# Mixer weights laid out by pieces on the host, with high and low parts kept together in DRAM

## The chip, the cores and the metric

The kernel is one launch on one core of a Trainium2 chip. A core has a matrix engine (PE, with its weight loads listed as PEld), a vector engine (DVE), an activation engine (ACT), a general engine (POOL) and a queue engine (SP) that here issues every DMA. The metric is the device time of one execution in microseconds, lower is better.

## The reference, cut to what matters

```python
def reference(x, w_in, ..., w_up, w_down):
    h = x                                             # (1, 2048, 1024) float32
    mix = hybrid_mixer(rmsnorm(h, pre_mix_norm), w_in, ..., w_out)
    h = h + rmsnorm(mix, post_mix_norm)
    u = rmsnorm(h, pre_mlp_norm) @ w_up               # 1024 -> 4096
    m = jnp.square(jax.nn.relu(u)) @ w_down           # 4096 -> 1024
    return h + rmsnorm(m, post_mlp_norm)

def hybrid_mixer(h, w_in, ..., w_out):
    z = h @ w_in                                      # 1024 -> 3600 columns, then split
    o_a = chunked_gated_linear_attention(gq, gk, gv, decay from glr)   # 4 heads, dk 64, dv 128
    o_b = chunked_gated_linear_attention(silu(hq), 1 - f, hi, log(f))  # 4 heads, 128 x 128
    return concatenate([gated_norm(o_a, gg), gated_norm(o_b, hg)]) @ w_out
```

All of it is float32 in and out.

## The kernel before, in words

The precision of float32 is had from three fast matmuls. Every operand is split into a high part (`hi`, a rounded copy made on ACT) and a low part (`lo`, raw minus `hi`, on DVE or POOL), and `mm3` (L264) adds `hi*hi`, `hi*lo` and `lo*hi` into one PSUM bank. So lines L267, L268 and L269 come in threes.

The work has three stages. The mixer runs first (0 to about 1010 us): four blocks of 512 tokens, 0 to 3, each a pass over four "units" (pairs of heads, in the order 0, 2, 3, 1) and then the output projection. Then come the up projection (to about 1640 us) and the down projection, which both use a seven-product scheme and read operands that earlier stages stored in DRAM.

The mixer's weights pass through class `Weights` as 72 pieces per block, the same 72 for each block. A piece is 128 partitions by 512 columns (528 for unit 0's values, which carry 16 gate columns). A "chan" piece is four 128x128 squares of `w_in`, a "value" piece is 128 rows of two column ranges of 256 (and the 16 gate columns for unit 0), an "out" piece is 128 rows by 512 columns of `w_out`. `plan` fixes the order in which pieces are taken. `load` issues the DMAs: a raw piece into one of 4 `wr` buffers, at most 4 pieces ahead of the last one that was split (L62). `prep` makes a raw piece into `hi` (tile `w`) and `lo` (tile `wl`), 12 buffers each. In block 0 `prep` splits on ACT (L257) and on DVE or POOL (L258) and stores `lo` to DRAM (`w_low`, L94). In blocks 1 to 3 the raw piece is loaded again (L74), `lo` is loaded from `w_low` (L79) and `hi` is copied anew on ACT (L90).

A matmul group ends in one of 4 PSUM banks `zp`. ACT empties the banks: for values by L498 and L282 (and DVE L500 for the gate columns), for the output projection by L740 and L742. PE can start the next group only when a bank is free.

What sets the order: the kernel is written in program order, and a scheduler then places each engine's instructions by its own simulated time line, so the order on an engine is fixed at build time and each engine runs it strictly in order. An instruction that waits holds up all that stand behind it on its engine. All DMAs stand in one such order, SP's.

`up_raw` (L906) loads a 512x256 half of a group of `w_up` columns, `down_raw` (L1131) a part of `w_down`; both are DMAs with a view that gathers short rows.

Of the kernel before, what the change touches and what calls it, by code (L numbers as in the profile page):

```python
# [38 lines left out]

class Weights:  # L40
# [19 lines left out]
    def load(self):  # L60
        y = self.layer
        while self.loaded < len(self.plan) and self.loaded < self.split + self.RAW:  # L62
            i, kept = self.loaded, self.loaded >= PIECES
            if kept and i >= self.freed + self.LIVE:
                return
            views, chan, _ = self.plan[i]
            raw = y.wp.tile([P, WM], F32, tag="wr", name=y.name("wr"), bufs=self.RAW)
            at = 0
            for v in views:
                n = v.shape[-1] * (4 if chan else 1)  # L70
                dst = raw[:, at:at + n]
                if chan:
                    dst = dst.rearrange("p (k n) -> p k n", n=P)
                y.nc.sync.dma_start(dst, v)  # L74
                at += n
# [4 lines left out]
            self.loaded += 1  # L80

    def prep(self):
        self.load()
# [1373 lines left out]
```

## Time and profile before

| | us |
|---|---|
| median of 3 runs (lowest, highest) | 2303.49 (2301.09, 2305.54) |
| the profiled execution, its own time | 2301.36 |
| its span, first to last instruction | 2299.6 |
| PE busy | 2227.0 (97%) |
| ACT busy | 1170.7 (51%) |
| DVE busy | 1414.0 (61%) |
| DMA moved | 419.20 MB, 182 GB/s over the span |

PE is busy for 97% of the span, so the span is PE's work plus about 72 us in which PE stood still. Most of these stand at the two ends of the span. The rest are waits of a few microseconds each, and the granted clock shows what each leaves behind: after some of them PE runs at less than its full clock for some microseconds.

### The profile page before, as it was taken

To read this page: it belongs to the slowest core of one execution; us is meant where nothing else is said; L and a number is where in the kernel's file an instruction comes from. 1 tells how busy PE (TensorE), PEld (TensorE's weight loads), DVE (VectorE), ACT (ScalarE), POOL (GpSimd) and SP (SyncE) were. 2 spreads that over 40 slices of the span, in tenths; PEclk is the share of its full clock that TensorE was granted. 3 is DMA by queue.
4 is the path that set the end of the run, shared out by engine and by line. 5 is a ranking of instruction groups with operands and counts; after the bars stand their busy time and mean duration, and the time that the engine had idled before them with its cause. 6 is when DMAs were issued, how large, how long until landed. Compare 5 with 4: busy or idle time off the path is not lost.

```text
span 2299.6 us, 31616 instructions
## 1 busy us (share of the span) xinstructions
PE 2227.0 (97%) x10922; PEld 1837.7 (80%) x10922; DVE 1414.0 (61%) x2272; ACT 1170.7 (51%) x2269; POOL 615.2 (27%) x418
## 2 busy tenths in 40 slices
PE   6999999999999999998999999999999999999995
PEld 5788788888888878877888878888778878888884
DVE  4666446433653475357865686655536876777688
ACT  4664576545764676456655565555543332233242
POOL 3331101001000130025633343232322333233265
PEclk9999999999999999999999999999999999999998
DMA  8545685368654994567944474443434342434265
GB/s 271 183 147 174 215 284 157 127 205 269 198 156 148 321 303 147 184 211 264 321 160 151 165 238 169 151 151 142 169 130 133 128 134 95 138 129 137 95 203 189
DMA packets 336235, 419.20 MB, mean 182 GB/s; under 512 B 30384, under 2 KB 219072, under 8 KB 336064
## 3 DMA queue, kind: packets, MB, share of 16 engines
q1 hardware_dynamic: 336064, 417.08, 55.3%
q8 instruction: 88, 1.44, 0.3%
q14 instruction: 83, 0.68, 0.1%
HBM read 299.47 MB, written 117.51 MB: 181 GB/s over the span
## 4 chain that ended last, share of the span: by engine, by line
PE 47%; DVE 3%; DMA 2%; issue 1%; ACT 1%; POOL 0%; SPq 0%; DVEq 0%; ACTq 0%; POOLq 0%
PE Y_f L1308 3%; PE Y_f L1309 3%; PE Y_f L1310 3%; PE Y_f L1013 3%; PE Y_f L1012 3%; PE Y_f L1014 3%; PE X_f L1308 2%; PE X_f L1310 2%; PE X_f L1309 2%; PE Z_f L1308 2%; PE Z_f L1309 2%; PE Z_f L1310 2%; PE Z_f L1013 2%; PE Z_f L1012 2%; PE Z_f L1014 2%; PE X_f L1014 2%
## 5 line engine op out<-in xcount | busy, mean ns | idle before, releaser
L267 PE MATMUL zp_f<-w_f,act_f 128*128 128x512 f32 (+2 forms) x896 | 328.6, 369 | 7.6 <-DVE gl_f L500 2.7
L268 PE MATMUL zp_f<-wl_f,act_f 128*128 128x512 f32 (+2 forms) x896 | 325.1, 363 | 0.2 <-POOL wl_f L258 0.2
L269 PE MATMUL zp_f<-w_f,act_f 128*128 128x512 f32 (+2 forms) x896 | 324.0, 364 | 0.0
L897 ACT ACTIVATE u_f<-raw_f 128x1024 fp32r<-128x1024 f32 x111 | 117.7, 1061 | 331.1 <-PE Y_f L1309 211.9
L276 POOL TENSOR_TENSOR rs_f<-ms_f,c_neghalf 128x1 f32<-128x1 f32 (+1 forms) x80 | 65.6, 827 | 752.1 <-DVE ms_f L274 752.0
L891 POOL TENSOR_TENSOR u_f<-raw_f,u_f 128x1024 fp32r<-128x1024 f32 x55 | 135.4, 2462 | 302.0 <-ACT u_f L897 301.0
L267 PEld LDWEIGHTS zp_f<-w_f,act_f 128*128 128x128 f32 x896 | 169.1, 190 | 35.2 <-issue 2.9
L90 ACT ACTIVATE w_f<-wr_f 128x512 fp32r<-128x512 f32 (+1 forms) x216 | 132.8, 630 | 119.2 <-DMA wr_f<-in_w_in 67.6
L269 PEld LDWEIGHTS zp_f<-w_f,act_f 128*128 128x128 f32 x896 | 169.6, 189 | 25.9 <-issue 0.7
L268 PEld LDWEIGHTS zp_f<-wl_f,act_f 128*128 128x128 f32 x896 | 170.0, 190 | 24.4 <-POOL wl_f L258 0.4
L1308 PE MATMUL Y_f<-act_f,u_f 128*128 128x512 f32 x384 | 150.2, 394 | 12.4 <-DVE acc_f L1267 10.4
L267 PE MATMUL zp_f<-act_f,w_f 128*128 128x512 f32 x384 | 152.8, 402 | 3.1 <-ACT act_f L257 3.1
L268 PE MATMUL zp_f<-act_f,w_f 128*128 128x512 f32 x384 | 151.7, 395 | 2.4 <-DVE act_f L258 2.4
L269 PE MATMUL zp_f<-act_f,wl_f 128*128 128x512 f32 x384 | 151.5, 395 | 0.0
L1309 PE MATMUL Y_f<-act_f,u_f 128*128 128x512 f32 x384 | 150.6, 392 | 0.0
L1310 PE MATMUL Y_f<-act_f,u_f 128*128 128x512 f32 x384 | 150.0, 392 | 0.0
L1267 DVE TENSOR_TENSOR acc_f<-acc_f,Y_f 128x1024 f32<-128x1024 f32 (+1 forms) x89 | 107.1, 1204 | 67.0 <-PE Y_f L1310 65.9
L897 ACT ACTIVATE w_f<-t_f 128x512 fp32r<-128x512 f32 x128 | 79.9, 628 | 108.0 <-PE Y_f L1013 55.1
L1014 PE MATMUL X_f<-act_f,w_f 128*128 128x512 f32 x256 | 100.0, 391 | 3.1 <-DVE w_f L894 2.5
L894 DVE TENSOR_TENSOR w_f<-t_f,w_f 128x512 fp32r<-128x512 f32 x96 | 79.9, 833 | 37.2 <-ACT w_f L897 37.2
L1012 PE MATMUL Y_f<-act_f,w_f 128*128 128x512 f32 x256 | 100.7, 393 | 1.8 <-DVE ev_f L1032 1.5
L1032 DVE TENSOR_TENSOR ev_f<-Y_f,p_f 128x512 f32<-128x512 f32 x94 | 64.6, 687 | 60.5 <-PE Y_f L1014 60.5
(261 smaller groups left out, 5752.5 us busy)
## 6 DMA issues: line engine op xcount, KB each, us to landing
raw_f<-u_operands SPq DMA_DIRECT2D x224, 256.0 KB, 3.0
u_operands<-ev_f SPq DMA_DIRECT2D x223, 256.0 KB, 2.1
wl_f<-w_low SPq DMA_DIRECT2D x192, 256.0 KB, 4.1
wr_f<-in_w_in SPq DMA_DIRECT2D x256, 128.0 KB, 3.7
wr_f<-in_w_up SPq DMA_DIRECT2D x62, 512.0 KB, 3.7
wr_f<-in_w_in SPq DMA_DIRECT2D x96, 256.0 KB, 4.5
wide_f<-in_x SPq DMA_DIRECT2D x32, 512.0 KB, 6.1
w_low<-wl_f SPq DMA_DIRECT2D x64, 256.0 KB, 3.4
```

The source lines that it names most:

```text
L90: y.nc.scalar.activation(hi, raw, AF.Copy)
L267: mm(out, a[0], b[0], start=i == 0, stop=False)
L268: mm(out, a[0], b[1], start=False, stop=False)
L269: mm(out, a[1], b[0], start=False, stop=i == n - 1)
L891: nc.gpsimd.tensor_tensor(out, a, b, op)
L897: self.nc.scalar.activation(hi, raw, AF.Copy)
L1012: mm(z, whi[:, k, :], hi, start=first and k == 0, stop=False, skip_group_check=more)
L1013: mm(z, whi[:, k, :], lo, start=False, stop=False, skip_group_check=more)
L1014: mm(z, wlo[:, k, :], hi, start=False, stop=end, skip_group_check=more)
L1308: mm(zx, hi[:, k, tok], whi, start=not loaded and k == 0, stop=False, skip_group_check=loaded)
L1309: mm(zx, hi[:, k, tok], wlo, start=False, stop=False, skip_group_check=loaded)
L1310: mm(zx, lo[:, k, tok], whi, start=False, stop=k == 1, skip_group_check=loaded)
```

## The change

On the host, `_layout` writes the 72 pieces one after the other into a new input `w_mix` (72, 128, 528), each in the form in which it stands in SBUF, and stores `w_up` and `w_down` so that the DMAs of `up_raw` and `down_raw` read one row of 4 KB per partition. In the kernel a piece's `hi` and `lo` are now the two halves of one tile `w` [128, 2, 576], and `w_split` (72, 128, 2, 528) replaces `w_low`. In block 0 a raw piece is one DMA from `w_mix`, split as before, and then both parts are stored in one DMA. In blocks 1 to 3 a piece is one DMA that brings both parts from `w_split` into its tile: no raw buffer and no work on ACT, and its only limit is that one of the 12 tiles is free (the limit of 4 raw pieces is left for block 0). The order of the buffers in the up stage's pool is another too.

```diff
+def pieces():
+    ...
+    for u in UNITS:
+        if u < 2:
+            chan(GQ + u * P, GK + u * P)
+    ...
+        out.extend(("value", k * P, cols) for k in range(KT))
+    for half in range(2):
+        out.extend(("out", k * P, [(half * 512, 512)]) for u in UNITS for k in (2 * u, 2 * u + 1))
+    return out
...
-    def part(self, tag, n):
+    def part(self):
         y = self.layer
-        return y.wp.tile([P, WS], F32R, tag=tag, name=y.name(tag), bufs=self.LIVE)[:, :n]
+        return y.wp.tile([P, 2, WS], F32R, tag="w", name=y.name("w"), bufs=self.LIVE)
...
     def load(self):
         y = self.layer
-        while self.loaded < len(self.plan) and self.loaded < self.split + self.RAW:
-            i, kept = self.loaded, self.loaded >= PIECES
-            if kept and i >= self.freed + self.LIVE:
-                return
-            views, chan, _ = self.plan[i]
-            raw = y.wp.tile([P, WM], F32, tag="wr", name=y.name("wr"), bufs=self.RAW)
-            at = 0
-            for v in views:
-                ...
-                y.nc.sync.dma_start(dst, v)
-                at += n
-            self.raw[i] = raw[:, :at]
-            if kept:
-                self.lo[i] = self.part("wl", at)
-                y.nc.sync.dma_start(self.lo[i].bitcast(F32), self.low[i % PIECES, :, :at])
+        while self.loaded < len(self.plan):
+            i = self.loaded
+            n = self.plan[i][0]
+            if i < PIECES:
+                if i >= self.split + self.RAW:
+                    return
+                raw = y.wp.tile([P, WM], F32, tag="wr", name=y.name("wr"), bufs=self.RAW)[:, :n]
+                y.nc.sync.dma_start(raw, y.io["w_mix"][i, :, :n])
+                self.raw[i] = raw
+            else:
+                if self.split < i or i >= self.freed + self.LIVE:
+                    return
+                z = self.part()
+                y.nc.sync.dma_start(z[:, :, :n].bitcast(F32), self.store[i % PIECES, :, :, :n])
+                self.give(z)
             self.loaded += 1
 
     def prep(self):
         self.load()
         y, i = self.layer, self.split
-        ...
-        if i in self.lo:
-            lo = self.lo.pop(i)
-            y.nc.scalar.activation(hi, raw, AF.Copy)
-        else:
-            lo = self.part("wl", n)
-            y.split(hi, lo, raw, eng=getattr(y.nc, self.plan[i][2]))
-            y.nc.sync.dma_start(self.low[i, :, :n], lo.bitcast(F32))
-        ...
+        if i in self.raw:
+            raw, z = self.raw.pop(i), self.part()
+            n = raw.shape[-1]
+            y.split(z[:, 0, :n], z[:, 1, :n], raw, eng=getattr(y.nc, self.plan[i][2]))
+            y.nc.sync.dma_start(self.store[i, :, :, :n], z[:, :, :n].bitcast(F32))
+            self.give(z)
+            self.load()
...
     def up_raw(self, g, half, r):
-        r = r.rearrange("p (k n) -> p k n", k=4)
-        view = self.io["w_up"][half * 512:half * 512 + 512, g * 256:g * 256 + 256]
-        self.nc.sync.dma_start(r, view.rearrange("(k p) n -> p k n", p=P))
-        return r
+        self.nc.sync.dma_start(r, self.io["w_up"][g, half])
+        return r.rearrange("p (k n) -> p k n", k=4)
...
-        self.nc.sync.dma_start(raw.rearrange("p (k n) -> p k n", k=2), view[f][:, :, h * 512:h * 512 + 512])
+        self.nc.sync.dma_start(raw, self.io["w_down"][kb, f, h])
         return raw
```

The lines of the changed kernel have other numbers (L257 becomes L283, L498 L496, L282 L308, L740 L738, L742 L740, L94 L122, L74 L105; the new load of both parts is L111).

The first place is on ACT, at the end of block 0, where the banks of the first half of the output projection are emptied (`zp` to `wide` and `ct`). Before:

```order
L257 ACTIVATE w_f_2608<-wr_f_2484 128x512
L257 ACTIVATE w_f_2617<-wr_f_2491 128x512
L90 ACTIVATE w_f_2644<-wr_f_2588 128x512
L90 ACTIVATE w_f_2646<-wr_f_2597 128x512
L90 ACTIVATE w_f_2670<-wr_f_2613 128x512
L740 ACTIVATE wide_f_2341<-zp_f_2363 128x512
L742 ACTIVATE ct_f_2538,ssm_f_2345<-zp_f_2363 128x512
L740 ACTIVATE wide_f_2342<-zp_f_2444 128x512
L742 ACTIVATE ct_f_2547,ssm_f_2346<-zp_f_2444 128x512
```

And in the changed kernel at the same place:

```order
L283 ACTIVATE w_f_2489<-wr_f_2376 128x512
L283 ACTIVATE w_f_2493<-wr_f_2382 128x512
L738 ACTIVATE wide_f_2238<-zp_f_2258 128x512
L740 ACTIVATE ct_f_2429,ssm_f_2242<-zp_f_2258 128x512
L738 ACTIVATE wide_f_2239<-zp_f_2337 128x512
L740 ACTIVATE ct_f_2438,ssm_f_2243<-zp_f_2337 128x512
```

The three copies L90 of the first pieces of block 1, which stood ahead of the first bank's emptying, are gone.

The second place is on ACT too, in unit 0 of block 0, where the first two pairs of value banks are emptied (`zp` to `wide`). Before:

```order
L257 ACTIVATE w_f_423<-wr_f_386 128x528
L257 ACTIVATE w_f_467<-wr_f_398 128x512
L257 ACTIVATE w_f_474<-wr_f_405 128x512
L498 ACTIVATE wide_f_341<-zp_f_344 128x256
L282 ACTIVATE wide_f_342<-zp_f_433 128x256
L498 ACTIVATE wide_f_341<-zp_f_466 128x256
L282 ACTIVATE wide_f_342<-zp_f_519 128x256
```

And in the changed kernel:

```order
L283 ACTIVATE w_f_395<-wr_f_363 128x528
L496 ACTIVATE wide_f_328<-zp_f_331 128x256
L308 ACTIVATE wide_f_329<-zp_f_404 128x256
L283 ACTIVATE w_f_438<-wr_f_372 128x512
L496 ACTIVATE wide_f_328<-zp_f_437 128x256
L308 ACTIVATE wide_f_329<-zp_f_486 128x256
```

The copies of the next unit's first two pieces (128x512) stood ahead of both pairs of banks; now the first pair stands ahead of them, and one copy stands between the pairs.

The third place is SP's order where unit 0's value pieces are loaded in block 0 (`wr` loads) and its first pieces are stored. Before:

```order
L94 DMA w_low<-wl_f_256 128x512
L74 DMA wr_f_260<-in_w_in 128x256
L74 DMA wr_f_260<-in_w_in 128x16
L74 DMA wr_f_260<-in_w_in 128x256
L94 DMA w_low<-wl_f_265 128x512
```

And in the changed kernel:

```order
L122 DMA w_split<-w_f_254 256x1x512
L105 DMA wr_f_258<-in_w_mix 128x528
L122 DMA w_split<-w_f_260 256x1x512
L105 DMA wr_f_264<-in_w_mix 128x528
L122 DMA w_split<-w_f_290 256x1x512
```

A value piece of unit 0 takes two places in SP's order where it took four, and its store carries twice the bytes. From the end of the mixer's last block on, PE's, ACT's, DVE's and POOL's orders are the same in both kernels.

## Rows read from the trace of the kernel before

**Rows 1.** The page's first part: busy time, share of the span and count of each engine; and from its second part PE's busy tenths in 40 slices of the span.

```profile
PE 2227.0 (97%) x10922; PEld 1837.7 (80%) x10922; DVE 1414.0 (61%) x2272; ACT 1170.7 (51%) x2269; POOL 615.2 (27%) x418
...
PE   6999999999999999998999999999999999999995
```

**Rows 2.** Stretches of the span in us: busy time and count of PE, PEld, DVE, ACT and POOL, then PE's granted clock, the share of the DMA engines' time and GB/s.

```profile
400.00:600.00 200.00, 200.00 (x1125) 167.39 (x1124) 90.70 (x227) 114.77 (x263) 10.86 (x12) 1.00 0.66 208
...
1000.00:1100.00 100.00, 89.55 (x387) 69.56 (x386) 77.97 (x99) 61.26 (x113) 47.52 (x36) 0.98 0.77 256
...
1400.00:1600.00 200.00, 200.00 (x884) 165.62 (x883) 121.75 (x170) 103.70 (x169) 61.17 (x44) 1.00 0.42 149
```

**Rows 3.** PE's waits by the instruction that ended them: us in total, times, longest.

```profile
PE zp_f L267 <- DVE gl_f L500: 2.7, 1, 2.7
PE zp_f L267 <- ACT ct_f L742: 2.6, 1, 2.6
PE X_f L1014 <- DVE w_f L894: 2.5, 3, 1.0
...
PE zp_f L267 <- ACT w_f L257: 1.1, 1, 1.1
...
PE zp_f L267 <- ACT w_f L90: 0.8, 1, 0.8
```

**Rows 4.** ACT's time line at the end of block 0: start, duration, line, tiles, and in brackets the idle time before it and what ended it.

```profile
249.77 0.63 ACT L90 ACTIVATE w_f<-wr_f 128x512 fp32r<-128x512 f32 x1 [2.43 <-DMA wr_f<-in_w_in]
251.96 0.63 ACT L90 ACTIVATE w_f<-wr_f 128x512 fp32r<-128x512 f32 x1 [1.56 <-DMA wr_f<-in_w_in]
252.50 0.58 ACT L740 ACTIVATE wide_f<-zp_f 128x512 f32<-128x512 f32 x1
252.98 0.59 ACT L742 ACTIVATE ct_f<-zp_f 128x512 f32<-128x512 f32 x1
```

**Rows 5.** PE's time line at the same place.

```profile
249.87 0.39 PE L269 MATMUL zp_f<-w_f,act_f 128*128 128x512 f32 x1
250.10 1.05 PE L419 MATMUL at_f<-ct_f,c_ones 128*128 128x128 f32 x8
253.71 0.79 PE L267 MATMUL zp_f<-w_f,act_f 128*128 128x512 f32 x1 [2.56 <-ACT ct_f L742]
254.30 0.63 PE L268 MATMUL zp_f<-wl_f,act_f 128*128 128x512 f32 x1
...
256.43 0.53 PE L267 MATMUL zp_f<-w_f,act_f 128*128 128x512 f32 x1
256.80 0.39 PE L268 MATMUL zp_f<-wl_f,act_f 128*128 128x512 f32 x1
```

**Rows 6.** ACT's time line in unit 0 of block 0.

```profile
45.03 0.63 ACT L257 ACTIVATE w_f<-wr_f 128x512 fp32r<-128x512 f32 x1 [2.75 <-DMA wr_f<-in_w_in]
46.56 0.63 ACT L257 ACTIVATE w_f<-wr_f 128x512 fp32r<-128x512 f32 x1 [0.89 <-DMA wr_f<-in_w_in]
47.09 0.36 ACT L498 ACTIVATE wide_f<-zp_f 128x256 f32<-128x256 f32 x1
```

**Rows 7.** PE's time line at the same place, and then two stretches around it in the form of rows 2.

```profile
44.73 0.28 PE L269 MATMUL zp_f<-w_f,act_f 128*128 128x256 f32 x1
47.72 0.39 PE L267 MATMUL zp_f<-w_f,act_f 128*128 128x272 f32 x1 [2.71 <-DVE gl_f L500]
...
48.00:52.00 4.00, 4.00 (x22) 4.00 (x22) 1.69 (x5) 3.14 (x10) 3.12 (x3) 0.57 1.00 306
52.00:56.00 4.00, 4.00 (x36) 3.98 (x35) 0.17 (x1) 0.96 (x3) 0.00 (x0) 1.00 0.78 230
```

**Rows 8.** SP's time line at the start: start and time to issue, and the count of DMAs in the row.

```profile
7.29 3.19 SPq L74 DMA_DIRECT2D wr_f<-in_w_in  x4
...
15.39 1.13 SPq L910 DMA_DIRECT2D st_f<-in_w_up  x2
16.57 2.33 SPq L409 DMA_DIRECT2D ct_f<-in_xT  x4
```

**Rows 9.** Two more waits of PE in its time line, in the mixer's first 40 us.

```profile
26.09 0.50 PE L268 MATMUL zp_f<-act_f,w_f 128*128 128x512 f32 x1 [0.57 <-DVE act_f L258]
39.50 0.51 PE L267 MATMUL zp_f<-w_f,act_f 128*128 128x272 f32 x2 [1.13 <-ACT w_f L257]
```

**Rows 10.** Block 0's first stretches in the form of rows 2.

```profile
0.00:20.00 20.00, 5.86 (x15) 4.14 (x16) 11.72 (x29) 10.75 (x18) 8.10 (x12) 1.00 0.92 279
20.00:40.00 20.00, 18.23 (x103) 15.37 (x103) 10.94 (x21) 7.77 (x14) 5.39 (x4) 1.00 0.88 278
40.00:60.00 20.00, 17.05 (x126) 16.63 (x125) 3.96 (x12) 10.00 (x25) 6.81 (x6) 0.91 0.73 221
60.00:80.00 20.00, 20.00 (x93) 15.70 (x92) 9.10 (x18) 13.69 (x27) 10.01 (x8) 1.00 0.87 275
80.00:100.00 20.00, 17.77 (x116) 13.64 (x116) 19.76 (x40) 12.35 (x25) 5.41 (x4) 0.99 0.78 251
100.00:120.00 20.00, 20.00 (x89) 15.60 (x89) 11.12 (x40) 15.54 (x48) 4.63 (x5) 0.92 0.03 9
```

**Rows 11.** The groups of instructions that the change takes away or alters: ACT's copies (count, busy us, mean ns, idle before them), and SP's stores of low parts in the first 100 us (durations in ns to issue, first and last start).

```profile
L90 ACT ACTIVATE w_f<-wr_f 128x512 fp32r<-128x512 f32 (+1 forms) x216 | 132.8, 630 | 119.2 <-DMA wr_f<-in_w_in 67.6
...
L94 SPq DMA_DIRECT2D w_low<-wl_f x32: 326/376/1415, 19.7 to 90.7; - x32
```

More of the change, by code (lines that the diff above doesn't have):

```diff
@@ L37, with chan @@
 GQ, GK, GV, GG, GLR, HQ, HF, HI, HG = 0, 256, 512, 1024, 1536, 1552, 2064, 2576, 3088
+UNITS = (0, 2, 3, 1)
+def pieces():
+    out = []
+    def chan(*cols):
+        out.extend(("chan", half * 512, [(col, P)]) for half in range(2) for col in cols)
+    for u in UNITS:
+        if u < 2:
+            chan(GQ + u * P, GK + u * P)
+        else:
+            for h in (2 * u - 4, 2 * u - 3):
+                chan(HF + h * P)
+                chan(HQ + h * P)
+        v, g = (GV, GG) if u < 2 else (HI, HG)
+        cols = [(v + u % 2 * 256, 256)] + [(GLR, 16)] * (u == 0) + [(g + u % 2 * 256, 256)]
+        out.extend(("value", k * P, cols) for k in range(KT))
+    for half in range(2):
+        out.extend(("out", k * P, [(half * 512, 512)]) for u in UNITS for k in (2 * u, 2 * u + 1))
+    return out
 class Weights:
@@ L57, in part, with give @@
+    def part(self):
         y = self.layer
-        return y.wp.tile([P, WS], F32R, tag=tag, name=y.name(tag), bufs=self.LIVE)[:, :n]
+        return y.wp.tile([P, 2, WS], F32R, tag="w", name=y.name("w"), bufs=self.LIVE)
+    def give(self, z):
+        n, chan, _ = self.plan[self.split]
+        hi, lo = z[:, 0, :n], z[:, 1, :n]
+        if chan:
+            hi, lo = (x.rearrange("p (k n) -> p k n", n=P) for x in (hi, lo))
+        self.parts[self.split] = (hi, lo)
+        self.split += 1
     def load(self):
@@ L84, in prep, with pump @@
         y, i = self.layer, self.split
-        raw = self.raw.pop(i)
-        n = raw.shape[-1]
-        hi = self.part("w", n)
-        if i in self.lo:
-            lo = self.lo.pop(i)
-            y.nc.scalar.activation(hi, raw, AF.Copy)
-        else:
-            lo = self.part("wl", n)
-            y.split(hi, lo, raw, eng=getattr(y.nc, self.plan[i][2]))
-            y.nc.sync.dma_start(self.low[i, :, :n], lo.bitcast(F32))
-        if self.plan[i][1]:
-            hi, lo = (z.rearrange("p (k n) -> p k n", n=P) for z in (hi, lo))
-        self.parts[i] = (hi, lo)
-        self.split += 1
+        if i in self.raw:
[5 more added lines that the diff above has]
+            self.load()
+    def pump(self, n):
         self.load()
-    def pump(self, n):
-        while n and self.split < len(self.plan) and self.split - self.freed < self.LIVE:
+        while n and self.split < PIECES and self.split - self.freed < self.LIVE:
             self.prep()
@@ L347, in mixer @@
                 self.spawn(self.combine(0, halves))
-            for u in self.UNITS:
+            for u in UNITS:
                 if u == 3 and b + 1 < NBLK:
@@ L731, in out_proj @@
         ss = [self.t([P, 2], "ssm", bufs=8) for _ in range(NCH)]
-        heads = [2 * u + h for u in self.UNITS for h in range(2)]
+        heads = [2 * u + h for u in UNITS for h in range(2)]
         def part(z, t, w, ks):
@@ L1419, in _layout @@
     out["hgrn_lower_bounds"] = np.ascontiguousarray(a["hgrn_lower_bounds"].reshape(2, 4, P).transpose(2, 1, 0))
-    out["w_out"] = a["w_out"][0]
+    out["w_mix"] = np.zeros((PIECES, P, WM), np.float32)
+    for i, (kind, row, cols) in enumerate(pieces()):
+        w = a["w_out" if kind == "out" else "w_in"][0][row:row + (512 if kind == "chan" else P)]
+        w = np.concatenate([w[:, c:c + n] for c, n in cols], axis=1)
+        w = w.reshape(-1, P, w.shape[1]).transpose(1, 0, 2).reshape(P, -1)
+        out["w_mix"][i, :, :w.shape[1]] = w
     for k in ("pre_mix_norm", "pre_mlp_norm"):
```

71 lines of the change are left out of this document (22 added, 49 removed).

## The prediction

> **What bounds the kernel now.** I read the page's first two parts first. PE is busy for 2227.0 of 2299.6 us and at nine tenths or more in nearly every slice; the two that fall well below are the first and the last [rows 1]. PE's work itself does not change: the changed kernel has the same matmuls. So the change can win or lose only in the some 72 us in which PE stands still, and in the stretches at low clock that follow such a stop.
>
> Second I read PE's stretches. Blocks in the middle of the mixer have nothing to win: in 400 to 600 us PE is busy for 200.00 of 200 [rows 2]. The 100 us around the change from mixer to up projection have 10.45 us idle. Third I read PE's waits by releaser [rows 3]: the long ones with a bank of the mixer are single events, 2.7 us (gate columns, L500) and 2.6 us (the output projection's emptying, L742), and there are 1.1 and 0.8 us in which PE waits for a copied weight piece. Fourth, the time lines at these places, to see why the releaser was late.
>
> At 250 us it is late because of ACT's order. ACT stood 2.43 and then 1.56 us idle for raw pieces of block 1 (L90), and only behind the third copy, at 252.50, did it empty the first bank (L740, L742) [rows 4]. PE had finished that half at about 250.1, did a small matmul, and then stood for 2.56 us [rows 5]. When it went on, its matmuls started 0.43 us apart, as from 254.30 to 256.43 (five steps, 2.13 us), and 0.23 us apart before. At 45 us it is the same: ACT waits 2.75 us for the raw piece that it copies at 45.03 and 0.89 us for the one at 46.56, and empties the banks from 47.09 [rows 6], while PE's last matmul of that group began at 44.73 and the next at 47.72; in 48 to 52 us the granted clock is 0.57, a mean of mostly the lower level (1.2 GHz) and a rest at 2.4 GHz [rows 7].
>
> **The change, part by part.**
>
> *Copies of blocks 1 to 3.* 216 copies L90 go, 132.8 us of ACT [rows 11]. Nearly all of it lies beside PE's work and is worth nothing by itself. What counts is the order. At the end of block 0 the three copies in front of L740 are gone, so ACT can empty the first bank as soon as PE leaves it. At the latest that is 249.87 + 0.39 = 250.26, the two ACT instructions take 0.58 + 0.59, and the bank is free by 251.4; the small matmul ends at 250.10 + 1.05 = 251.15. At most 0.3 us of the 2.56 stay. With the stop the low clock goes too: from 253.71 to 256.80 stand 7 steps that took 3.09 us and would take 7 x 0.23 = 1.6. Term A: -(2.4 + 1.5) = -3.9 us. Its cover is that the next group finds its weights, which are pieces of block 0, split already. What is late next is block 1's input: by SP's order two loads of x (512 KB each) now stand ahead of most xT loads, about 1.05 MB at some 330 GB/s (an estimate between 149/0.42 = 355 and 279/0.92 = 303 of rows 2 and 10), 3 us. PE comes to block 1 only behind the second half, 4 x 24 matmuls x 0.23 = 22 us later, so I price that at nothing.
>
> The wait of 0.8 us for an L90 copy goes with the copies [rows 3]. Term B: -0.8.
>
> *First emptying in unit 0.* The two copies 128x512 no longer stand ahead of the first pair of banks. ACT can start at about 45.0, when PE's group ends, in place of 47.09. Between L498's start and PE's resumption lie 47.72 - 47.09 = 0.63 us, so some 0.65 of 2.71 stay: -2.05. After the 1.13 us stop at 39.5 [rows 9] no low clock is seen at once, so I take the low stretch to go with the stop: 0.57 for 4.0 us is 1.7 us lost, of which I count 1.4. Term C: -3.4 us; bounds 0 (the last value piece comes later by as much) and -4.4.
>
> *Issue on SP at the start.* Four raw loads of 512-byte rows take 3.19 us to issue, two of `w_up` 1.13, four of xT with 2 KB rows 2.33 [rows 8]. With rows of 2 and 4 KB I take 0.4 to 0.58 each, so the xT loads stand 1 to 2 us earlier. PE's 0.57 us wait for a late `hn` [rows 9] goes. The first matmul does not move, since it waits for x and its statistics. Term D: -0.5.
>
> *Stores twice as large in block 0.* Each of 72 pieces stores 262 KB more. In the first 100 us stand 32 stores [rows 11], 8.4 MB more, 25 us at 330 GB/s. The DMA engines are busy for 0.92, 0.88, 0.73, 0.87 and 0.78 of those 100 us [rows 10], so 16.4 us are free: 9 us short. Longer rows give back some: 32 loads of 262 KB at 303 GB/s take 28 us, at 355 24. About 5 us are short, and the next 20 us, at 0.03, take them up. Whether PE feels it depends on the 12 pieces of lead. In 60 to 80 us the DMA share is 0.87 and PE is busy for 20.00 of 20, so pieces may come late without a stop. Bounds: -1.1 (the piece wait of rows 9 goes) and +11 (all 9 us reach PE, and 2 us of low clock with them). I take +1.5, near the row of 60 to 80. Term E: +1.5.
>
> First what the rows say on row length: 400 to 600 us, with rows of 0.5, 1 and 2 KB, moves 208 GB/s at a share of 0.66 (315 GB/s if it were full); 1400 to 1600 us, 1 and 2 KB, moves 149 at 0.42 (355) [rows 2]. The Trainium skill (DMA: Bandwidth & Descriptors, Specifications) puts the least transfer for line rate at 512 B, so by it the reshaping gives nothing back and only the extra bytes count. By that rule term E would be nearer +5 and the sum -5; the rows differ from it by about a tenth, and the measurement decides.
>
> *Loads in blocks 1 to 3.* One DMA of 512 KB in place of two to four with the same bytes. The raw half could come 4 pieces early before, and now both halves wait for the tile's last reader, 256 KB more behind each release, 0.8 us at 330 GB/s. That is small against a lead of 12 pieces of 2.7 us each (12 matmuls x 0.23), and the share of 0.66 falls. Zero, bounds -1 and +4.
>
> *`w_up` and `w_down`.* In 1000 to 1100 us PE idles 10.45 us, mostly in waits for DVE's and ACT's preparation of up weights and operands. DVE is at 78% there, and its order is unchanged. Shorter issue and transfer of four `w_up` loads may bring a microsecond. Term F: -1.0, bounds -5 (half the idle time) and +3 (the other buffer order holds a first load back).
>
> *Order elsewhere in the mixer.* The scheduler's small moves are worth 0 with +-3.
>
> Sum: -3.9 - 0.8 - 3.4 - 0.5 + 1.5 - 1.0 = -8.1 us. Against the profiled execution's own 2301.4 (span 2299.6 and 1.8 around it) that is 2293.3. The median of the runs shown is 2.1 above that execution, which lies inside their spread, so the forecast for the median is 2303.5 - 8.1 = 2295.4.
>
> **The rivals.**
>
> R1, the waits are passed on: ACT empties in time, but PE then stops for a late piece or `hn` at the same two places. For it: the stop at 45 us lies where the DMA engines are full (share 1.00, 306 GB/s in 48 to 52 [rows 7]), and there they get more bytes. Against it: at 250 us the next 22 us of weights are in SBUF. A would keep half (-2) and C nothing, with B, D, E and F as above: -2 - 0.8 - 0.5 + 1.5 - 1 = -2.8, or 2300.7.
>
> R2, slower: the stores hold the start back. The place is block 0 up to the third unit. Stores stand ahead of loads on SP and in the DMA engines, so each piece waits for 524 KB of the piece before. It decides if pieces come slower than PE's 2.7 us per piece for longer than the lead lasts; at 786 KB per piece that is below 786/2.7 = 290 GB/s, and the first 80 us moved 221 to 279 GB/s with the shares above [rows 10]. Then E is +11 and C is lost: -3.9 - 0.8 - 0.5 + 11 - 1 = +4.8, or 2308.3. Against it: full engines gave 306 GB/s [rows 7].
>
> R3, the change of stage gains as well: larger `w_up` rows come when PE waits for the chain behind them, F -5, E zero: -13.6, or 2289.9. Against it: DVE's order there does not move.
>
> That the change doesn't do what it says (both parts not stored for all blocks, copies still there) is excluded by the orders.
>
> **How the numbers follow.** A difference of 0.2%, 4.6 us, is about what can be told from none. Forecast 0.52 (its own range 2291 to 2299.5), R1 0.25 (2298 to 2304), R2 0.12 (2304 to 2312), R3 0.11 (2286 to 2291). Faster is below 2298.9: 0.49 of the forecast's 0.52, 0.03 of R1's, all of R3's, 0.63. Slower is above 2308.1: about half of R2 and a little for what I have not seen, 0.08. The rest, 0.29, is the same. The range runs over R3's middle to R2's lower part, 2288 to 2306, with 0.2 outside.
>
> **What would show it right or wrong.** A: no stop above 0.5 us between the halves of block 0's output projection and clock 1.00 behind it. C: PE's stop at the first values below 1 us, no clock near 0.57. E: PE busy in 20 to 100 us at least as long as before (73.05 us), DMA share above 0.9. F: 1000 to 1100 us with 8 to 11 us idle. Wrong would be: a new stop at a weight piece in block 0, waits for `w` loads in blocks 1 to 3, or the same idle time at other places.

## The result and the profile after

The changed kernel takes 2288.77 us (median of 6 runs, 2282.82 to 2290.67) against 2303.74 for the kernel before (6 runs, 2298.42 to 2305.54): a ratio of 0.9937, interval 0.9926 to 0.9949. The gain is 15.0 us where 8.1 was forecast; 2288.77 lies 0.8 us inside the lower end of the range. The profiled execution took 2288.09 us, with a span of 2286.1, 13.5 us under the span before; the readings below add up to these 13.5.

The page's first part, a row of its second and the memory traffic from its third, of the kernel after:

```profile
PE 2223.8 (97%) x10922; PEld 1835.7 (80%) x10922; DVE 1412.2 (62%) x2272; ACT 1057.2 (46%) x2053; POOL 618.3 (27%) x418
...
PE   7999999999999999998999999999999999999995
...
HBM read 299.47 MB, written 136.45 MB: 191 GB/s over the span
```

ACT lost 113.5 us of busy time and PE 3.2 [rows 1]: what ACT is spared is, as expected, not what the kernel is spared.

To see where the 13.5 us come from I follow one kind of PE instruction through the time line of both kernels: the first transposes of a head group (L589, after the change L587), the first transposes of a block's activations by L826 (L824), and the first up matmul. The kernel before, then the kernel after:

```profile
117.57 0.38 PE L589 MATMUL at_f<-c_ident,ct_f 128*128 128x128 f32 x2
...
240.79 0.49 PE L589 MATMUL at_f<-c_ident,ct_f 128*128 128x128 f32 x3
...
287.86 0.60 PE L826 MATMUL at_f<-c_ident,wide_f 128*128 128x128 f32 x4
...
779.22 0.60 PE L826 MATMUL at_f<-c_ident,wide_f 128*128 128x128 f32 x4
...
985.67 0.49 PE L589 MATMUL at_f<-c_ident,ct_f 128*128 128x128 f32 x3
...
1019.14 0.50 PE L1012 MATMUL X_f<-act_f,w_f 128*128 128x512 f32 x1
```

```profile
110.35 0.38 PE L587 MATMUL at_f<-c_ident,ct_f 128*128 128x128 f32 x2
...
232.31 0.49 PE L587 MATMUL at_f<-c_ident,ct_f 128*128 128x128 f32 x3
...
275.22 0.60 PE L824 MATMUL at_f<-c_ident,wide_f 128*128 128x128 f32 x4
...
765.21 0.60 PE L824 MATMUL at_f<-c_ident,wide_f 128*128 128x128 f32 x4
...
968.11 0.49 PE L587 MATMUL at_f<-c_ident,ct_f 128*128 128x128 f32 x3
...
1001.58 0.50 PE L1008 MATMUL X_f<-act_f,w_f 128*128 128x512 f32 x1
```

| stretch of the kernel before | forecast for it | measured |
|---|---|---|
| start to 118 us | C, D and E: -2.4 | -7.2 |
| 118 to 241 | 0 | -1.3 |
| 241 to 288, output projection of block 0 | A: -3.9 | -4.2 |
| 288 to 779, blocks 1 and 2 | 0 | -1.4 |
| 779 to 986, block 3 | B: -0.8 (its stop lies at 783) | -3.5 |
| 986 to 1019 | 0 | 0.0 |
| up and down projections | F: -1.0 | +4.1 |

**The start.** Stretches of the kernel after, in the columns of rows 10:

```profile
20.00:40.00 20.00, 19.61 (x115) 17.44 (x114) 11.02 (x21) 8.21 (x15) 5.22 (x5) 1.00 1.04 380
40.00:60.00 20.00, 19.36 (x142) 18.13 (x143) 4.88 (x14) 12.23 (x30) 10.25 (x8) 1.00 1.02 365
60.00:80.00 20.00, 20.00 (x86) 15.61 (x85) 12.97 (x27) 13.48 (x27) 5.96 (x5) 1.00 0.86 305
80.00:100.00 20.00, 19.42 (x125) 14.28 (x123) 19.81 (x51) 12.34 (x27) 7.35 (x5) 1.00 0.89 294
100.00:120.00 20.00, 20.00 (x123) 16.14 (x124) 11.44 (x29) 17.03 (x50) 8.63 (x8) 1.00 0.66 245
...
48.00:52.00 4.00, 4.00 (x35) 4.00 (x34) 0.08 (x1) 1.82 (x5) 1.78 (x3) 1.00 1.05 389
52.00:56.00 4.00, 4.00 (x36) 3.96 (x35) 0.94 (x3) 2.01 (x5) 2.64 (x3) 1.00 1.02 361
```

PE is busy for 78.4 us of 20 to 100 where it was 73.05 [rows 10]; the clock of 0.57 in 48 to 52 us is now 1.00 [rows 7]. The DMA engines move more: 380 and 365 GB/s in 20 to 60 us, where the kernel before moved 278 and 221. ACT's time line at the first values:

```profile
43.30 0.39 ACT L496 ACTIVATE wide_f<-zp_f 128x256 f32<-128x256 f32 x1 [1.43 <-PE zp_f L295]
43.58 0.38 ACT L308 ACTIVATE wide_f<-zp_f 128x256 f32<-128x256 f32 x1
43.84 0.63 ACT L283 ACTIVATE w_f<-wr_f 128x512 fp32r<-128x512 f32 x1
```

ACT now waits for PE there, not for a raw piece, and the emptying (L496) comes before the next piece's split (L283) [rows 6].

**Block 0's output projection.** ACT's time line, then PE's, in the kernel after:

```profile
240.69 0.60 ACT L738 ACTIVATE wide_f<-zp_f 128x512 f32<-128x512 f32 x1 [4.79 <-PE zp_f L295]
241.18 0.59 ACT L740 ACTIVATE ct_f<-zp_f 128x512 f32<-128x512 f32 x1
```

```profile
241.39 0.39 PE L295 MATMUL zp_f<-w_f,act_f 128*128 128x512 f32 x1
241.62 0.83 PE L417 MATMUL at_f<-ct_f,c_ones 128*128 128x128 f32 x6
242.21 0.48 PE L293 MATMUL zp_f<-w_f,act_f 128*128 128x512 f32 x1
```

ACT empties the first bank as soon as PE frees it (the bracket names PE), and PE goes from one half to the next without an idle time in brackets [rows 4, 5].

**Block 3.** Here the kernel before had stops that my rows had not covered. PE's time line of the kernel before, and 780 to 840 us in the columns of rows 2:

```profile
783.29 0.40 PE L267 MATMUL zp_f<-w_f,act_f 128*128 128x272 f32 x1 [0.84 <-ACT w_f L90]
787.61 0.39 PE L267 MATMUL zp_f<-w_f,act_f 128*128 128x272 f32 x1 [0.40 <-ACT ct_f L436]
...
803.39 0.66 PE L826 MATMUL at_f<-c_ident,wide_f 128*128 128x128 f32 x4 [2.07 <-DVE wide_f L820]
```

```profile
780.00:840.00 60.00, 56.69 (x381) 49.40 (x381) 28.54 (x63) 43.16 (x88) 11.46 (x10) 1.00 1.03 347
```

The same 60 us of the kernel after, and then the same work, which now stands 14 us earlier:

```profile
780.00:840.00 60.00, 59.09 (x350) 48.24 (x349) 41.20 (x98) 39.89 (x92) 17.23 (x15) 1.00 0.86 306
766.00:826.00 60.00, 60.00 (x405) 52.59 (x404) 32.48 (x74) 38.53 (x77) 11.52 (x10) 1.00 1.02 362
```

The DMA engines are full for 60 us (1.03), as in no other stretch after the start that I had read, and PE idles 3.3 us. After the change the same work finds them as full (1.02), but they move 362 GB/s in place of 347, and PE does not stop.

### The profile page after: what moved, and what is told of

Same layout as the page of the kernel before. It is cut to its first block, busy times and chain, and to the rows that moved or that the text cites. A ratio compares the mean times of both kernels' runs of the same rounds, so it can differ in the third digit from the quotient of the medians.

```text
span 2286.1 us, 30635 instructions
## 1 busy us (share of the span) xinstructions
PE 2223.8 (97%) x10922; PEld 1835.7 (80%) x10922; DVE 1412.2 (62%) x2272; ACT 1057.2 (46%) x2053; POOL 618.3 (27%) x418
## 4 chain that ended last, share of the span: by engine, by line
PE 48%; DVE 3%; DMA 1%; issue 1%; ACT 1%; POOL 0%; SPq 0%; DVEq 0%; ACTq 0%; POOLq 0%
PE Y_f L1008 4%; PE Y_f L1303 4%; PE Y_f L1009 4%; PE Y_f L1010 3%; PE Y_f L1304 3%; PE Y_f L1305 3%; PE X_f L1303 2%; PE X_f L1304 2%; PE X_f L1305 2%; PE Z_f L1303 2%; PE Z_f L1304 2%; PE Z_f L1305 2%; PE Z_f L1010 2%; PE Z_f L1008 2%; PE Z_f L1009 2%; PE X_f L1008 2%
## 5 line engine op out<-in xcount | busy, mean ns | idle before, releaser
L293 PE MATMUL zp_f<-w_f,act_f 128*128 128x512 f32 (+2 forms) x896 | 325.1, 367 | 0.4 <-ACT w_f L283 0.4
L294 PE MATMUL zp_f<-w_f,act_f 128*128 128x512 f32 (+2 forms) x896 | 323.9, 362 | 0.6 <-POOL w_f L284 0.6
L295 PE MATMUL zp_f<-w_f,act_f 128*128 128x512 f32 (+2 forms) x896 | 321.8, 362 | 0.0
L293 PEld LDWEIGHTS zp_f<-w_f,act_f 128*128 128x128 f32 x896 | 167.1, 188 | 27.4 <-issue 2.7
L295 PEld LDWEIGHTS zp_f<-w_f,act_f 128*128 128x128 f32 x896 | 168.4, 188 | 25.1 <-issue 0.9
L294 PEld LDWEIGHTS zp_f<-w_f,act_f 128*128 128x128 f32 x896 | 168.5, 188 | 24.9 <-POOL w_f L284 0.8
L1303 PE MATMUL Y_f<-act_f,u_f 128*128 128x512 f32 x384 | 150.9, 396 | 12.8 <-DVE acc_f L1262 10.4
L293 PE MATMUL zp_f<-act_f,w_f 128*128 128x512 f32 x384 | 152.7, 401 | 2.9 <-ACT act_f L283 2.9
L294 PE MATMUL zp_f<-act_f,w_f 128*128 128x512 f32 x384 | 152.0, 396 | 1.9 <-DVE act_f L284 1.9
L295 PE MATMUL zp_f<-act_f,w_f 128*128 128x512 f32 x384 | 151.7, 395 | 0.0
L1303 PE MATMUL X_f<-act_f,u_f 128*128 128x512 f32 x252 | 99.3, 394 | 2.8 <-ACT act_f L895 2.0
```

The costliest lines, as they stand in the source:

```text
L293: mm(out, a[0], b[0], start=i == 0, stop=False)
L294: mm(out, a[0], b[1], start=False, stop=False)
L295: mm(out, a[1], b[0], start=False, stop=i == n - 1)
L1303: mm(zx, hi[:, k, tok], whi, start=not loaded and k == 0, stop=False, skip_group_check=loaded)
```

## The experiments

Theory 1: the gain is ACT's order, copies out of the way of full banks. Theory 2: it is the DMA side, rows of 2 KB and more and fewer DMAs. Theory 3: it is chance, another order of everything else. The table gives every kernel's shift against the kernel before at the places of the first table (one profiled execution each, us; minus is earlier), and then its median and its ratio to runs of the kernel before on the same chip.

| kernel | 118 | 241 | 288 | 779 | 986 | median | ratio, interval |
|---|---|---|---|---|---|---|---|
| after | -7.2 | -8.5 | -12.6 | -14.0 | -17.6 | 2288.8 | 0.9937, 0.9926 to 0.9949 |
| e1 | -3.9 | -3.9 | -4.2 | -3.1 | -7.8 | 2289.6 | 0.9956, 0.9941 to 0.9970 |
| e2 | -2.7 | -3.2 | -7.4 | -8.8 | -12.8 | 2291.6 | 0.9956, 0.9941 to 0.9970 |
| e3 | -1.4 | -1.4 | -3.4 | -1.6 | +0.5 | 2303.1 | 1.0001, 0.9990 to 1.0012 |
| e4 | -6.0 | -7.3 | -11.4 | -12.8 | -16.5 | 2286.3 | 0.9927, 0.9910 to 0.9944 |
| e5 | -5.7 | -7.0 | -10.6 | -9.9 | -14.2 | 2293.2 | 0.9957, 0.9943 to 0.9971 |
| e6 | -1.2 | -1.2 | -5.2 | -5.7 | -2.1 | 2299.9 | 0.9992, 0.9977 to 1.0006 |
| e7 | -5.2 | -5.6 | -9.8 | -11.2 | -13.2 | 2290.4 | 0.9938, 0.9920 to 0.9956 |
| e8 | -1.7 | -0.3 | -4.5 | -5.9 | -9.9 | 2292.5 | 0.9950, 0.9932 to 0.9968 |
| e9 | -6.6 | -6.6 | -10.8 | -11.7 | -11.7 | 2291.8 | 0.9956, 0.9939 to 0.9972 |
| e10 | -7.3 | -8.5 | -12.6 | +27.6 | +50.6 | 2350.4 | 1.0206, 1.0189 to 1.0223 |
| e11 | +1.6 | +10.1 | +10.4 | +22.4 | +18.8 | 2318.5 | 1.0070, 1.0053 to 1.0086 |
| e12 | -7.6 | -8.9 | -13.0 | +18.6 | +41.4 | 2347.4 | 1.0196, 1.0175 to 1.0217 |

How far one execution's start can be trusted shows in kernels whose block 0 is the same: before, e3 and e6 stand at 0 to -1.4 in the first column, after, e5, e10 and e12 at -5.7 to -7.6, e1 and e9 at -3.9 and -6.6. Differences of under 2 to 3 us there mean nothing. The stretch from 241 to 288 repeats far better: it takes 42.9 to 43.4 us in ten of the kernels, and 47.1, 46.8 and 45.1 in before, e1 and e3, which keep the copies on ACT; e11, which waits for pieces from 260 us on, is apart. Before, e1 and e3 all have the stop between the two halves of the output projection (2.56, 1.99 and 1.91 us). The low clock behind it is in before and e1 only: the granted clock of the 10 us around the stop (250 to 260, 246 to 256 and 249 to 259 us) is 0.83, 0.83 and 1.00 (0.83 is a mean of the levels 2.4 and 1.2 GHz). So the stop itself costs 1.9 to 2.6 us at this place, and 1.6 to 1.9 more come only when the clock falls, which it did in two of these three executions.

A profile can also lie to one side of its kernel's runs: e1's (2295.6) is one of its three longest executions, while the other five of eight took 2288.9 to 2289.6, and e5's (2288.3) is its fastest.

**e1, e2: each half of the mixer's change alone.** e1 is the kernel before with the raw pieces laid out by the host, one DMA each, and with low parts and copies as before:

```diff
-            at = 0
-            for v in views:
...
-                y.nc.sync.dma_start(dst, v)
-                at += n
+            at = sum(v.shape[-1] * (4 if chan else 1) for v in views)
+            y.nc.sync.dma_start(raw[:, :at], y.io["w_mix"][i % PIECES, :, :at])
```

> The kernel before with one part of the change: raw pieces come as one DMA of long rows from w_mix, in all four blocks; low parts alone are stored, ACT copies the high part in blocks 1 to 3, w_up and w_down as before. Theory 1 (the gain is ACT's order: copies out of the way of emptied banks): only the start gains, 2 to 4 us, ratio 0.998 to 0.999, and PE still stops for 2 to 3 us between the halves of block 0's output projection. Theory 2 (the gain is the DMA engines' rate with long rows): 8 to 12 us, ratio near 0.996, the first values' banks emptied 4 us earlier and up projection begun near 1009 us (before 1019.1, changed kernel 1001.6). Theory 3 (chance of the scheduler's new order): anything between, with the stops at new places.

e2 is the changed kernel with raw pieces loaded as before (one to three DMAs with short rows), and the old `w_up` and `w_down`:

```diff
-                y.nc.sync.dma_start(raw, y.io["w_mix"][i, :, :n])
+                for c0, m in cols:
+                    if kind == "chan":
...
+                        y.nc.sync.dma_start(raw.rearrange("p (k n) -> p k n", n=P), v)
+                    else:
+                        y.nc.sync.dma_start(raw[:, at:at + m], src[row:row + P, c0:c0 + m])
```

> The changed kernel with raw pieces of block 0 loaded by short rows from w_in and w_out as before, and w_up and w_down as before; both parts stored and loaded together. Theory 1: 9 to 12 us faster than before, ratio near 0.9955, no stop between the halves of block 0's output projection. Theory 2: the start is slower than before (twice the stores, no faster rows), first values' banks emptied at 47 us or later, and the whole within 4 us of before, ratio 0.998 to 1.001. Theory 3: no stop at 250 us but stops elsewhere.

By the ratios either half alone is worth about 10 us of the changed kernel's 14.5, so the halves overlap; both gain all of block 3's 3.5 us. Elsewhere they gain at different places. e2 gains 4.2 us between 241 and 288, e1 only 0.3 there. e1 gains 3.9 at the start with the old order on ACT. Its ACT time line, and PE's:

```profile
43.32 0.63 ACT L277 ACTIVATE w_f<-wr_f 128x512 fp32r<-128x512 f32 x1 [0.71 <-DMA wr_f<-in_w_mix]
43.86 0.37 ACT L518 ACTIVATE wide_f<-zp_f 128x256 f32<-128x256 f32 x1
```

```profile
44.49 0.39 PE L287 MATMUL zp_f<-w_f,act_f 128*128 128x272 f32 x1 [0.47 <-DVE gl_f L520]
```

The split (L277) still stands ahead of the emptying (L518), but its raw piece lands earlier, and PE stops for 0.47 us in place of 2.71 [rows 6, 7]. e2 has short rows and the larger stores, and still its start is not longer (-2.7 at 118 us), where theory 2 had it slower than before. Both kernels lose block 3's stops: PE is busy there for 60.00 and 59.72 us of 780 to 840. The order of the instructions there is new in both, so theory 3 is not excluded for this block.

**e3, e4: `w_up` and `w_down` alone, and undone.** e3 is the kernel before with these two; e4 is the changed kernel without them:

```diff
-        r = r.rearrange("p (k n) -> p k n", k=4)
-        view = self.io["w_up"][half * 512:half * 512 + 512, g * 256:g * 256 + 256]
-        self.nc.sync.dma_start(r, view.rearrange("(k p) n -> p k n", p=P))
-        return r
+        self.nc.sync.dma_start(r, self.io["w_up"][g, half])
+        return r.rearrange("p (k n) -> p k n", k=4)
```

> The kernel before with w_up and w_down alone laid out in long rows. Theories 1 and 2 as far as the mixer goes: no change there, 1 us or less at the change of stage, ratio 0.999 to 1.0005. Theory 2 taken further (rows count wherever DMAs are read): 3 us or more at the change of stage, idle there down from 10 to 7 us, ratio 0.9985 or less. Theory 3: the mixer's order is untouched, so nothing.

> The changed kernel with w_up and w_down as before. Theories 1 and 3: the same as the changed kernel within 2 us, ratio to before 0.993 to 0.995, up projection begun at 1001 to 1002 us. Theory 2 taken further: 3 us or more of the gain are lost, ratio 0.995 to 0.996.

They do nothing: e3's interval holds 1, and e4's overlaps that of the changed kernel. From the first up matmul to the end of the span the six kernels before, after and e1 to e4 take 1279.2 to 1284.5 us (e2 the least, after the most, e3 1281.8), in no order by these rows, and all fourteen take 1278.7 to 1285.6. The +4.1 us of the first table is of that size, so no cause is claimed for it.

**e5, e6: ACT's copies put back, and moved away.**

```diff
                 y.nc.sync.dma_start(z[:, :, :n].bitcast(F32), self.store[i % PIECES, :, :, :n])
+                raw = y.wp.tile([P, WM], F32, tag="wr", name=y.name("wr"), bufs=self.RAW)[:, :n]
+                y.nc.scalar.activation(raw, z[:, 0, :n].bitcast(F32), AF.Copy)
                 self.give(z)
```

> The changed kernel, and in blocks 1 to 3 ACT copies the loaded high half of every piece once more into a raw tile that nobody reads: 216 copies of some 0.63 us, as before, with the new loads, stores and row lengths kept. Theory 1 (ACT's order, the gain at block 0's end comes from the copies that stood ahead of the emptying): a stop of 2 to 4 us comes back between the halves of block 0's output projection with low clock behind it, the transposes at block 0's end (275.2 us in the changed kernel) come at 278 to 281, and the time is 2292 to 2296. Theory 2 (the DMA side gives the gain) and theory 3 (chance of order): no stop there, 2287 to 2291; by theory 3 the third and fourth block may move by 4 us either way.

```diff
-            y.nc.scalar.activation(hi, raw, AF.Copy)
+            y.nc.gpsimd.tensor_copy(hi, raw)
```

> The kernel before, and the 216 copies of kept pieces' high half in blocks 1 to 3 stand on GpSimd in place of ACT; nothing else differs, the DMAs are those of before. Theory 1: the stop of 2.56 us at block 0's end goes with the low clock behind it, 2296 to 2299. Theory 2: 2302 to 2304, since loads and stores are as before. Theory 3: the copies move the order of everything, so block 3's 3.5 us may go as in the three kernels that gained there, whatever becomes of block 0's end. The first 100 us should move by under 2 us in theories 2 and 3; in theory 1 the stop at the first values shortens only if a copy stood ahead of it, which no copy of blocks 1 to 3 did.

e6 does at block 0's end what theory 1 says: 4.0 us earlier from 241 to 288, with the DMAs of before. Its time lines on ACT and GpSimd:

```profile
248.18 0.60 ACT L740 ACTIVATE wide_f<-zp_f 128x512 f32<-128x512 f32 x1 [5.02 <-PE zp_f L269]
```

```profile
250.40 0.62 POOL L90 CAST w_f<-wr_f 128x512 fp32r<-128x512 f32 x1 [1.56 <-DMA wr_f<-in_w_in]
```

Now GpSimd waits 1.56 us for the raw piece, and ACT does not. That e6 gains less in all than theory 1 had is block 3's doing, where it loses 3.6 us (below, with e9). As a whole it is not shown to be faster: its interval holds 1.

e5's median lies in theory 1's range, its place does not: the copies are back on ACT, and 241 to 288 takes only 0.5 us more than in the changed kernel. ACT's time line there:

```profile
242.48 0.63 ACT L113 ACTIVATE wr_f<-w_f 128x512 f32<-128x512 f32 x1 [5.05 <-DMA w_f<-w_split]
243.02 0.58 ACT L740 ACTIVATE wide_f<-zp_f 128x512 f32<-128x512 f32 x1
```

One copy stands ahead of the emptying, where the kernel before had three, and its piece landed at about the time when PE left the bank. So a copy's 0.63 us is not the cost; a copy that waits for a late piece, with an emptying behind it, is. Over the later blocks e5 pays more: its gain shrinks from 10.6 to 9.9 us between 288 and 779, where the changed kernel's grows from 12.6 to 14.0.

**e7, e8: the raw loads of block 0 in two DMAs,** by columns (rows of 1 KB), or by partitions (rows of 2 KB):

```diff
-                y.nc.sync.dma_start(raw, y.io["w_mix"][i, :, :n])
+                for c in (0, n // 2):
+                    y.nc.sync.dma_start(raw[:, c:c + n // 2], y.io["w_mix"][i, :, c:c + n // 2])
```

> The changed kernel, and in block 0 each raw piece is loaded by two DMAs of half its columns, so rows of 1 KB in place of 2 KB; bytes are the same. If row length makes the start faster (theory 2): 20 to 60 us move under 350 GB/s in place of 365 to 380 with the share still near 1, the start is 1 to 4 us later than in the changed kernel, 2290 to 2293. If the number of DMAs does (issue on SP), it is as late as the kernel with two DMAs by partitions. Theory 1: no difference, 2287 to 2290.

```diff
+                for c in (0, P // 2):
+                    y.nc.sync.dma_start(raw[c:c + P // 2, :], y.io["w_mix"][i, c:c + P // 2, :n])
```

> The changed kernel, and in block 0 each raw piece is loaded by two DMAs of 64 partitions, with rows of 2 KB as in the changed kernel: as many DMAs as the kernel split by columns, with rows twice as long. If row length counts: as the changed kernel, 2287 to 2290, 365 to 380 GB/s in 20 to 60 us. If the number of DMAs or their issue counts: 1 to 4 us later, like the kernel split by columns. Theory 1: no difference from the changed kernel in either.

In the profiles the halves with the longer rows are the worse ones: at 241 us e8 has kept 0.3 of 8.5 us, e7 5.6. The medians do not tell the two apart, their intervals overlap. With rows of 1 KB e7 moved 366 and 362 GB/s in 20 to 40 and 40 to 60 us, where theory 2 had under 350 and the changed kernel moved 380 and 365. So 2 KB against 1 KB is not what the start gains by. Rows of 512 bytes, and of 64 in the gate columns, which the kernel before loads too, were not tried by themselves against 1 KB, nor one DMA against three with the same rows; which of these lets the pieces land earlier stays open. e8's time line on ACT, and PE's, show what it loses by:

```profile
43.56 0.64 ACT L284 ACTIVATE w_f<-wr_f 128x528 fp32r<-128x528 f32 x1 [5.22 <-DMA wr_f<-in_w_mix]
```

```profile
44.26 1.25 PE L294 MATMUL zp_f<-w_f,act_f 128*128 128x272 f32 x4 [3.88 <-ACT w_f L284]
```

With the changed kernel's code everywhere else, a raw piece that lands late brings back a stop of 3.88 us in unit 0's value columns, this time for the piece itself, and low clock behind it (0.84 in 48 to 52 us). Why halves by partitions landed later there than halves by columns stays open.

**e9: long rows, and the copies on GpSimd.** Both edits of e1 and e6, on the kernel before.

> The kernel before with two edits: raw pieces of the mixer come in rows of 2 KB from the array laid out by pieces (as in the run with the rows alone), and the 216 copies of kept pieces stand on GpSimd in place of ACT. Only low parts are stored, both halves of a kept piece come by two DMAs as before. If ACT's order at block 0's end (4 us) and row length (3.9 us at the start, 3.5 to 4.7 us in block 3) are the whole of the gain, storing both parts together is not needed: transposes at block 0's end at 278 to 280.5 us (before 287.9, rows alone 283.6), first up matmul 13 us earlier than before, 2286 to 2291. If keeping both parts together has a gain of its own (fewer DMAs, no raw tile), it stays near the run with the rows alone: 2289 to 2294 and block 0's end after 281 us.

Up to 779 us it comes near to the changed kernel (-11.7 against -14.0) without keeping both parts together. In block 3 it gains nothing: 206.4 us from 779 to 986, as before, against 201.8 in e1. e6 is 3.6 us longer there than the kernel before, too. GpSimd's copies cost block 3 some 4 us, then. The traces show a part of the way; why DVE's instructions take longer beside these copies was not tested. DVE's busy time, with the same 2272 instructions, is 1432.9 us in e6 and 1432.4 in e9, against 1414.0 in before and 1413.4 in e1, and the longest stops of block 3 are waits for DVE:

```profile
PE at_f L722 <- DVE ct_f L710: 3.0, 2, 1.6
```

```profile
PE at_f L742 <- DVE ct_f L730: 1.7, 1, 1.7
```

These are e6 in 780 to 860 us, where the kernel before waits 1.1 us for the same, and e9 in 767 to 860, where e1 has no such wait.

**e10, e12: the kept pieces of blocks 1 to 3 in four DMAs,** by columns (rows of 512 bytes) and by partitions (rows of 2 KB):

```diff
-                y.nc.sync.dma_start(z[:, :, :n].bitcast(F32), self.store[i % PIECES, :, :, :n])
+                for c in range(0, n, n // 4):
+                    to, src = z[:, :, c:c + n // 4], self.store[i % PIECES, :, :, c:c + n // 4]
+                    y.nc.sync.dma_start(to.bitcast(F32), src)
```

> The changed kernel, and in blocks 1 to 3 each kept piece comes by four DMAs of a quarter of its columns, so rows of 512 bytes in place of 2 KB; bytes, order and block 0 are the same. If row length gave block 3's gain (theory 2): 780 to 840 us move 290 to 350 GB/s at full share in place of 366 to 393, PE stops in 765 to 850 us come back as in the kernel before (2 to 5 us), 2290 to 2296. If the new order of the engines gave it by chance (theory 3) or ACT's copies did (theory 1): no change there, 2287 to 2291. Blocks 1 and 2 stay by all theories, their DMA engines are two thirds full.

> The changed kernel, and in blocks 1 to 3 each kept piece comes by four DMAs of 32 partitions, with rows of 2 KB: as many DMAs as in the run with short kept rows (2350 us), rows four times as long. There SP issued 20 of them in a row in 12.97 us, 0.65 each, 2.6 us for a piece of which PE takes one in 2.7. If SP's issue makes that run slow: about the same here, 2330 to 2355, with PE stops for loads of kept pieces. If rows of 512 bytes make it slow: 2287 to 2300, and at full share the DMA engines move 350 GB/s and more where they moved 200 to 245 there.

e10's expectation missed by more than 50 us, in blocks 1 and 2 too, which no theory had. It had changed two things at once, and e12 tells them apart: with rows four times as long it is as slow. SP's time line of e10, of e12, and PE's waits of e12:

```profile
799.40 12.97 SPq L113 DMA_DIRECT2D w_f<-w_split  x20
```

```profile
790.34 25.38 SPq L113 DMA_DIRECT2D w_f<-w_split  x40
```

```profile
PE zp_f L295 <- DMA w_f<-w_split: 30.6, 19, 5.0
```

SP needs 0.65 and 0.63 us for one DMA, 2.5 to 2.6 for a piece, while PE takes a piece in 2.7. Whatever else SP has to issue then makes it late, and it can hardly catch up; this is worked out from the sizes, no run issued these loads from a second queue. The DMA engines were not full meanwhile: in 800 to 820 us their share is 0.85 and 0.80, with PE busy for 10.90 and 12.74 of 20 us. In the changed kernel a piece of 512 KB is one DMA, which SP issues in 0.52 us (median of 59 in 300 to 500 us). The number of DMAs per piece sets this cost, not the row length.

**e11: each piece of block 0 stored twice.**

```diff
             y.nc.sync.dma_start(self.store[i, :, :, :n], z[:, :, :n].bitcast(F32))
+            y.nc.sync.dma_start(self.store[PIECES + i, :, :, :n], z[:, :, :n].bitcast(F32))
```

> The changed kernel, and in block 0 each piece is stored a second time, to an array that nobody reads: 72 more stores of some 525 KB, with which term E's cost is doubled and more. By the rival that was slower (stores hold the start back) pieces come later than PE takes them: PE stops at weight pieces from 40 us on, PE busy in 20 to 100 us falls from 78.4 to under 74, 2295 to 2315. If the lead of 12 pieces and the free share after 100 us take up this too, as the forecast had it for the first store: 2288 to 2293, under 3 us lost by 118 us of the kernel before.

20 to 100 us of e11, and of the kernel after, in the columns of rows 2:

```profile
20.00:100.00 80.00, 72.17 (x412) 59.70 (x411) 36.77 (x82) 37.92 (x78) 19.46 (x15) 0.96 1.02 376
```

```profile
20.00:100.00 80.00, 78.40 (x463) 65.45 (x461) 48.69 (x111) 46.26 (x97) 28.79 (x21) 1.00 0.95 336
```

The rival that was slower is real, one store further on: 30 us more than the changed kernel, and 3.5 more than the upper end that the expectation had for it. The changed kernel's share of 0.95 says how little room it has left.

## Why the prediction was right, and where it was wrong

**Right in sign and in two of its places, half in size.** That the time lies in the range is in part luck: in the profiled execution the gain up to the first up matmul is 17.6 us, where the range ended at 15.5, and the later stages, which gave back 4.1 us for no cause that the runs show, brought it inside. A: forecast -3.9, measured -4.2, and e6 and e9 show its cause with the copies alone. The place has no stop and no low clock now, as was to be seen if A held. Its size was right for this execution of the kernel before; where the clock did not fall (e3) the place held only 2.2 us. B: the stop it names is gone, at 783 us, but e1 keeps the copies and loses it too, so the copies' going is not shown to be the reason. D: xT's loads were issued at 15.63 in place of 16.57, and the wait at 26.09 is gone; the first four raw loads took 2.90 us to issue, not four times 0.4 to 0.58, so that term had its size from a wrong step.

**C was right in what went and half right in why.** The stop at the first values and its low clock are gone. I put it down to the copies' place in ACT's order. e1 keeps that place and has 0.47 us left of the stop, e8 has the new place and waits 3.88 us for a piece: what decides there is when the raw pieces land.

**E charged PE with a cost that did not come.** C, D and E together were -2.4 and measured -7.2. None of the three is measured alone, but with C at its bound of -4.4 and D as forecast E would still be -2.3, below its own bound of -1.1; the spread of the start, some 2 us, nearly covers that, so a gain by E is not shown, but a cost is not to be seen either. The engines did take up the larger stores as was worked out: they moved 380 and 365 GB/s in 20 to 60 us, and their share in 100 to 120 us rose from 0.03 [rows 10] to 0.66. But PE did not feel it: its busy time in 20 to 100 us rose by 5.3 us, and it waits 0.39 and 0.64 us for pieces near 40 us where it waited 1.13 [rows 9]. e2 shows the same with short rows: the stores of E are there, PE waits 1.74 us for a piece at 39.19, and the start is not later for it. By the rule of the Trainium skill (DMA: Bandwidth & Descriptors, Specifications) E stood nearer +5, further off still.

**"Loads in blocks 1 to 3: zero" failed.** I read 400 to 600 us for the middle of the mixer, and 1000 to 1100, and took the share of 0.66 for all three blocks. Block 3's first unit has the engines full and three stops in a row; it gave 3.5 us. Kernels with one DMA for a raw or kept piece gain there (e1 4.7 us, e2 4.1); whether it is the number of DMAs, the row length or the new order of the instructions was not separated in that block.

**F was nothing** (e3, e4), inside its bounds; in the 100 us around the change of stage (982.4 to 1082.4 after) PE idles 10.51 us, where it idled 10.45. R3's time, 2289.9, is near the measured one by a mechanism that did not occur. R1's stops at the two places did not come; e11 shows where R2 begins.

## What to carry to other kernels

An engine that both prepares weights and empties banks stops the matmul engine whenever a load that it waits for is late, and there are two cures, each enough at one place here: move the waiting instruction off that engine (block 0's end, e6), or let the load land earlier (the first values, e1). When a load is reshaped, count its DMAs first: splitting a 512 KB load in four cost 59 to 62 us here, and rows of 1 KB in place of 2 KB in block 0 1.6 us by the medians, less than the intervals tell. Before a stretch is priced at nothing, look at every stretch with the DMA engines' share near 1, not at a mean of three blocks.

## What the runs showed of the hardware

At a share near 1, the four us from 48 to 52 moved 306 GB/s with raw rows of 0.5 KB (before [rows 7]), 374 with rows of 1 KB (e7) and 389 with 2 KB (after). I had expected a tenth between the ends. It looks like a quarter, but the stores of e7 and after carry twice the bytes, in rows of 2 KB as before. e2, with these stores and raw rows of 0.5 KB, moved 359 at a share of 1.07, where after moved 389 at 1.05: for the same share that is the tenth. The traces of before and after also hold the time of each packet, one row each, on its DMA engine. The medians over the whole execution are the same in both: 27 ns for 512 B, 46 for 1 KB, 84 for 2 KB and 159 for 4 KB, which for 16 engines is 303, 356, 390 and 412 GB/s. These times lie on a line of 38 ns per KB and 8 ns per packet (an estimate from the four medians). The Trainium skill (DMA: Bandwidth & Descriptors, Specifications) has line rate from 512 B up. These packets do not agree with that: rows of 512 B move at 78% of the rate of rows of 2 KB.

The time to issue a DMA on SP was 0.63 to 0.65 us in e10 and e12 for 128 to 132 KB, whatever its rows, and 0.52 for the 512 KB of the changed kernel. So the issuing queue alone held e10's loads to 135,168 bytes / 0.65 us = 208 GB/s; 800 to 820 us of e10 moved 216, stores and other loads included, at a share of 0.85.
